# Sparse attention: item scores as three 64-row products a head, two heads on the two halves of the array

## The chip, the cores and the metric

The kernel runs on one core of a Trainium2 chip. The metric is device time in microseconds for one execution; shown are the times of several executions, and the profile of one of them. Engine names in the rows: PE is TensorE's matmuls, PEld its weight loads, DVE VectorE, ACT ScalarE, POOL GpSimd, SP SyncE, which issues the transfers.

## The reference

Two decoder layers over 512 tokens of width 1024: the first mixes tokens with latent attention (MLA), the second with the sparse attention in which the change lies. Each layer then attends to 256 memory tokens and applies a SwiGLU FFN; every part ends in a residual and a layer norm. The sparse attention, cut to what matters:

```python
h = x @ w_in        # q: 16 heads of 64, k and v: 4 heads of 64, q_idx: 8 of 64, k_idx: 64, w_idx: 8
def one_block(args):                                    # 128 queries
    dots = jnp.einsum('bqhd,bkd->bqhk', qi_blk, k_idx) * (IDX_DIM ** -0.5)
    score = jnp.einsum('bqh,bqhk->bqk', wi_blk, jax.nn.relu(dots))
    score = jnp.where(causal[None], score, -jnp.inf)
    _, sel = lax.top_k(score, topk)                     # topk = 128
    k_sel, v_sel, pos_sel = (gather_rows(a, sel) for a in (k, v, pos))
    logits = jnp.einsum('bqngd,bqknd->bqngk', qg, k_sel) * (DSA_HEAD_DIM ** -0.5)
    logits = jnp.where(sel_ok[:, :, None, None, :], logits + bias, -jnp.inf)
    p = jax.nn.softmax(logits, axis=-1)
    return jnp.einsum('bqngk,bqknd->bqngd', p, v_sel).reshape(b, Q_BLOCK, 1024)
out = from_blocks(lax.map(one_block, ...)) @ w_o
```

All of it is float32. The kernel reaches that precision with products of split operands: a value is a high part (rounded to TensorE's fp32r) and a low part, the rest.

## The kernel before

The kernel doesn't gather. For each query tile `qt` (128 queries, 0 to 3) it scores all keys up to the tile's end, n = 128 (qt + 1) of them, adds -2^100 to those that the top-k search has not chosen, and takes the softmax over the row. Matmuls are at least 256 columns wide, so N is 256, 256, 384 and 512 for the four tiles.

An ordinary projection (`mm3`, L126 to L128) is three products of 128 rows: high by high, high by low, low by high.

The item scores differ. A head has only 64 dimensions, so half the array's 128 rows would be empty. `stack_q_pool` (L942) therefore stacks the two parts of one head in the 128 rows. It gets the projection of two heads in one bank, copies it to SBUF as `f` (L944), casts the high part of the even head into rows 0 to 63 of `QA` and that of the odd head into rows 64 to 127 of `QB` (L945, L946, ScalarE), and GpSimd subtracts the low parts into the other half of each (L947, L948). The keys stand in both halves: `KA[g]` holds the high part of kv head g twice, `KB[g]` its low part twice. One product of `Q` with `KA` and one with `KB` (L1059, L1060) give all four part products of one head, accumulated in one bank. For tiles 1 to 3 a product with the identity (`identr`, L1058) first puts the mask of the top-k search into the bank.

`dsa_scores(qt, g)` does this for the four query heads of kv head g, one bank each, and hands each bank to VectorE (bias and row minimum, L428) and ScalarE (exponential, L435). `dsa_t` (L1072) turns the weights with four 128x128 transposes for each key block and splits them; `dsa_pv` multiplies them with the values (L1093, L1094), normalises (transposes at L1104) and stores the result. VectorE's top-k search (`topk`, L1004 and L1005) is spread between the query projections. Queries are projected for two heads at a time, j = 0 to 7; the scores of tile 0 are run between these projections by the table `steps`, those of the other tiles in a loop that keeps scores, turning and values of neighbouring items (qt, g) in flight. The scheduler then puts the instructions of each engine into their order; engines run their own lists in order and wait for each other by semaphores. Scores use the four banks "b", transposes and values the four banks "a".

Elsewhere in the kernel a score has the other form: the index scores (L984) take three products of 64 rows, one head on rows 0 to 63 and the next on rows 64 to 127, each into its own bank:

```python
pss = [bank("b") for _ in range(2)]
for a, b in ((0, KIA), (0, KIB), (1, KIA)):
    for e in range(2):
        es = slice(64 * e, 64 * e + 64)
        nc.tensor.matmul(pss[e][:, :n], qi[a][es, ts_], b[es, :n], start=b is KIA and a == 0, stop=a == 1)
```

Of the kernel before, what the change touches and what calls it, by code (L numbers as in the profile page):

```python
# [11 lines left out]
F32 = mybir.dt.float32  # L12
# [3 lines left out]
ALU = mybir.AluOpType  # L16
# [52 lines left out]
def tile_hybrid_mla_dsa_deepnorm_block(ctx: ExitStack, tc: tile.TileContext, A: dict, out: bass.AP):  # L69
    nc = tc.nc  # L70
# [9 lines left out]
    def nm(s):  # L80
        uid[0] += 1
        return f"{s}_{uid[0]}"

    def t2(dt=F32, shape=(P, 512)):
        return tp.tile(list(shape), dt, tag="t2", name=nm("t2"), bufs=39)
# [7 lines left out]
    def bank(tag, shape=(P, 512)):  # L93
        return pp.tile(list(shape), F32, tag=tag, name=nm("ps"))
# [17 lines left out]
    def chunk(src, shape, eng=None, after=(None, None)):  # L112
        n = int(np.prod(shape[1:]))
        raw = wp.tile([P, 1024], F32, tag="raw", name=nm("raw"), bufs=3)
        with behind(after[0]):
            nc.sync.dma_start(raw[:, :n], src)
        h = wp.tile([P, 1024], FR, tag="wh", name=nm("wh"))
        l = wp.tile([P, 1024], FR, tag="wl", name=nm("wl"))
        split(h[:, :n], l[:, :n], raw[:, :n], eng, after[1])
        if len(shape) == 2:  # L120
            return h[:, :n], l[:, :n]
        k = shape[1]
        return (h[:, :n].rearrange("p (k m) -> p k m", k=k), l[:, :n].rearrange("p (k m) -> p k m", k=k))
# [11 lines left out]
    identr = cp.tile([P, P], FR, name="identr")  # L135
# [273 lines left out]
    def proj_tiles(ws, XT, halves):  # L409
        pss = [bank("a") for _ in ws]  # L410
        if halves:
            for cols in HALVES:
                for ps, w in zip(pss, ws):
                    proj(ps, w, XT, cols)
        else:
            for ps, w in zip(pss, ws):
                proj(ps, w, XT, (0, 512))
        return pss
# [32 lines left out]
    def ts_of(tt):  # L451
        return slice(P * tt, P * tt + P)
# [46 lines left out]
    for c in range(4):  # L499
        h, l = XT[c // 2]  # L500
        rx = raw_x[c // 2]
        step = 1 if c == 0 else 2
        for i in range(0, 2, step):
            k0 = 2 * (c % 2) + i
            split(h[:, k0:k0 + step], l[:, k0:k0 + step], rx[:, k0:k0 + step])
            if 2 * c + i in w_parts:
                t, a, b = w_parts[2 * c + i]
                split(whs[t][:, a:b], wls[t][:, a:b], raw_w[t][:, a:b])
        for i in range(2):
            k = 2 * c + i  # L510
            xh, xl = k_of(XT, k)
            for tt in range(NT):
                ts_ = ts_of(tt)
# [60 lines left out]
    for tt in range(NT):  # L574
        ps = bank("a")
# [363 lines left out]
    XT = norm.XT  # L939


    def stack_q_pool(ps, QA, QB):  # L942
        f = t2()
        nc.scalar.copy(f, ps)  # L944
        nc.scalar.copy(QA[0:64], ps[0:64])  # L945
        nc.scalar.copy(QB[64:128], ps[64:128])  # L946
        nc.gpsimd.tensor_tensor(QA[64:128], f[0:64], QA[0:64].bitcast(F32), op=ALU.subtract)  # L947
        nc.gpsimd.tensor_tensor(QB[0:64], f[64:128], QB[64:128].bitcast(F32), op=ALU.subtract)  # L948

    wvs = [chunk(A["w_vi"][:, NV * k0:NV * k1], (P, k1 - k0, NV)) for k0, k1 in ((0, 3), (3, 6), (6, 8))]  # L950
    VD = t8(FR, (P, 4, 4, P))
# [2 lines left out]
    for tt in range(NT):  # L954
        pv = bank("a")
        ts_ = slice(P * tt, P * tt + P)
# [13 lines left out]
    masks = [None] + [t2() for _ in range(1, NT)]  # L970
    for j in range(4):
        pq = bank("a")
# [3 lines left out]
        for qt in range(1, NT):  # L976
            n = P * (qt + 1)
            ts_ = slice(P * qt, P * qt + P)
            acc = masks[qt]
# [6 lines that stand above are left out]
                h = 2 * j + e  # L986
# [12 lines left out]
    def topk(qt, its):  # L999
        n = P * (qt + 1)  # L1000
        acc = masks[qt]
        for it in its:
            m8 = tp.tile([P, 8], F32, tag="m8", name=nm("m8"), bufs=4)
            nc.vector.max(out=m8, in_=acc[:, :n])  # L1004
            nc.vector.match_replace(out=acc[:, :n], in_to_replace=m8, in_values=acc[:, :n], imm_value=-3e38)  # L1005
        if its[-1] < TOPK // 8 - 1:
            return
        mk = MK[:, qt]
        nc.vector.tensor_scalar(mk[:, :n], acc[:, :n], -2e38, -BIG, op0=ALU.is_gt, op1=ALU.mult)
        masks[qt] = mk  # L1010
# [3 lines left out]
    KA, KB = [], []  # L1014
# [15 lines left out]
    def dsa_bias(qt, g):  # L1030
        n = P * (qt + 1)
        c0 = 127 + 384 - 128 * qt
        if (qt, g) == (1, 0):
            bts = [t2(F32, (P, 2, 256)) for _ in range(2)]
        else:
            bts = [t8(F32, (P, 4, 512)) if qt else t2(F32, (P, 4, P))]
        m = 4 // len(bts)
        for i, bt in enumerate(bts):
            read = nc.sync.dma_start(bt[:, :, 0:n],
                                     scr[bass.ds(r * (1 + qt), 1), 4 * g + m * i:4 * g + m * i + m, :,  # L1040
                                         c0:c0 + n].rearrange("a h p k -> p (a h) k"))
        reads.append(read)
        return [bts[i // m][:, i % m, 0:n] for i in range(4)]

    Q, OTd = [], {}
    q8 = t8()
    first_bias, reads, spreads, copies = [], [], [], []

    def dsa_scores(qt, g):
        n = P * (qt + 1)  # L1050
        N = max(n, 256)
        ts_ = slice(P * qt, P * qt + P)
        bt = dsa_bias(qt, g) if 4 * qt + g > 4 else first_bias[4 * qt + g]
        sx = Softmax(bt)
        for i in range(4):
            ps = bank("b")
            if qt:
                nc.tensor.matmul(ps[:, :N], identr, masks[qt][:, :N], start=True, stop=False)  # L1058
            nc.tensor.matmul(ps[:, :N], Q[4 * g + i][:, ts_], KA[g][:, :N], start=qt == 0, stop=False)  # L1059
            nc.tensor.matmul(ps[:, :N], Q[4 * g + i][:, ts_], KB[g][:, :N], start=False, stop=True)  # L1060
            sx.exp(i, ps[:, :n], 0.125, bt[i], copies[-1] if copies else None)
        return sx

    def dsa_t(qt, g, sx):
# [54 lines left out]
    def run_s(i):  # L1119
        if i < 16:  # L1120
            Ss[i] = dsa_scores(*items[i])
# [7 lines left out]
    def run(word):  # L1129
        kind, i = word[0], int(word[1:])  # L1130
        if kind == "p":
            dsa_pv(*items[i], *PT.pop(i))
        else:
            (run_s if kind == "s" else run_t)(i)

    for j in range(8):
        if j < 5:
            first_bias.append(dsa_bias(j // 4, j % 4))
        for _ in range(min(NTK, len(todo))):
            topk(*todo.pop(0))  # L1140
        (pq,) = proj_tiles([chunk(A["w_q"][j], (P, NK, P), nc.gpsimd)], XT, False)
        if j < 2:
            qa, qb = q8[:, 2 * j], q8[:, 2 * j + 1]
        else:
            qa, qb = t2(FR), t2(FR)
        stack_q_pool(pq, qa, qb)
        Q += [qa, qb]
        for word in steps.get(j, "").split():
            run(word)

# [5 lines left out]
    for i in range(3, 16):  # L1156
        a = 1 if i < LA else 0
# [99 lines left out]
```

## Time and profile before

| | |
|---|---|
| time, median of 3 runs | 1523.58 us (1523.28 to 1525.23) |
| the profiled execution: its time, its span | 1523.23 us, 1521.4 us |
| busy share PE, DVE, ACT, POOL | 98%, 65%, 43%, 20% |
| index scores, L984 (72 products of 64 rows) | 788.8 to 812.7 us |
| query projections and their splits (L944 first to L948 last) | 832 to 881.4 us |
| item scores, L1059 and L1060 (128 products of 128 rows) | 843.9 to 941.0 us |

The span runs from the first to the last instruction of the profile; the time is the device's own and a little longer. A matmul's row in the timeline gives its start and its duration; neighbours overlap, so the durations of a busy stretch add up to more than the stretch. Rows of the form `out<-in 128*128 128x512` give the rows and columns of the stationary operand and the shape of the moving one; `64*128` is a product on 64 of the 128 rows. Line numbers are those of the kernel before.

### The profile page before, as it was taken

The numbers are of one execution on the slowest core, as the hardware profiler recorded it, in microseconds if no ns is written. First come the engines' busy times: TensorE is split into PE (matmuls) and PEld (weight loads), VectorE is DVE, ScalarE is ACT, GpSimd is POOL, SyncE is SP. The second block draws the span as 40 slices with busy tenths as digits, with TensorE's granted clock in tenths as the row PEclk, the third lists the DMA queues.
The fourth block names the chain that finished last, engine by engine and source line by source line (L and its number), as shares of the span: only waits on it lengthen the run. The fifth ranks groups of instructions, "written<-read, shape, count | busy, mean of one in ns | idle before, by whom it ended". The sixth has DMA issues, their size and how long they took to land.

```text
span 1521.4 us, 20268 instructions
## 1 busy us (share of the span) xinstructions
PE 1491.2 (98%) x7666; PEld 1263.9 (83%) x7666; DVE 992.5 (65%) x1735; ACT 647.2 (43%) x1156; POOL 304.2 (20%) x299
## 2 busy tenths in 40 slices
PE   9999999999999999999999989999999999999997
PEld 8788888988898888888888778898888888888886
DVE  7887868554746655654568989675557555666545
ACT  4777753443233333333256588344422433333320
POOL 1322001000032331410024653000002232323002
PEclk9999999999999999999999999999999999999999
DMA  6234423432333233333243146343423233232321
GB/s 216 72 104 116 143 83 133 128 115 70 126 97 98 83 125 98 97 97 98 91 139 96 60 160 225 111 139 97 122 72 125 83 125 97 97 104 78 99 95 56
DMA packets 51143, 166.16 MB, mean 109 GB/s; under 512 B 5284, under 2 KB 11828, under 8 KB 48996
## 3 DMA queue, kind: packets, MB, share of 16 engines
q1 hardware_dynamic: 50468, 163.61, 33.1%
q8 instruction: 60, 0.98, 0.3%
q10 hardware_dynamic: 576, 1.25, 0.2%
q14 instruction: 39, 0.32, 0.1%
HBM read 160.60 MB, written 9.47 MB: 112 GB/s over the span
## 4 chain that ended last, share of the span: by engine, by line
PE 86%; DVE 8%; ACT 3%; issue 2%; DMA 1%; POOL 0%; POOLq 0%; SPq 0%; DVEq 0%; ACTq 0%
PE ps L126 26%; PE ps L127 26%; PE ps L128 26%; DVE t L104 2%; DVE t L1005 2%; DVE m L1004 2%; ACT t L435 1%; PE ps L344 1%; PE ps L1072 1%; ACT t L102 1%; PE ps L660 1%; DVE wl L104 1%; PE ps L984 1%; PE ps L786 0%; PE ps L1093 0%
## 5 line engine op out<-in xcount | busy, mean ns | idle before, releaser
L126 PE MATMUL ps<-t,wh 128*128 128x512 f32 (+2 forms) x1248 | 452.1, 362 | 5.8 <-DVE t L104 3.4
L127 PE MATMUL ps<-t,wh 128*128 128x512 f32 (+2 forms) x1248 | 450.2, 361 | 1.2 <-DVE t L104 1.2
L128 PE MATMUL ps<-t,wl 128*128 128x512 f32 (+2 forms) x1248 | 450.5, 361 | 0.0
L102 ACT CAST wh<-raw 128x1024 fp32r<-128x1024 f32 (+2 forms) x217 | 226.5, 1044 | 438.0 <-PE ps L127 157.7
L104 DVE TENSOR_TENSOR wl<-raw,wh 128x1024 fp32r<-128x1024 f32 (+2 forms) x196 | 252.5, 1289 | 209.6 <-ACT wh L102 208.2
L126 PE MATMUL ps<-wh,t 128*128 128x512 f32 (+3 forms) x774 | 295.4, 382 | 0.0
L127 PE MATMUL ps<-wl,t 128*128 128x512 f32 (+3 forms) x774 | 293.2, 379 | 0.1
L128 PE MATMUL ps<-wh,t 128*128 128x512 f32 (+3 forms) x774 | 292.8, 378 | 0.0
L126 PEld LDWEIGHTS ps<-t,wh 128*128 128x128 f32 x1248 | 235.5, 189 | 43.1 <-DVE t L104 5.6
L128 PEld LDWEIGHTS ps<-t,wl 128*128 128x128 f32 x1248 | 235.6, 189 | 36.3 <-issue 1.1
L127 PEld LDWEIGHTS ps<-t,wh 128*128 128x128 f32 x1248 | 235.6, 189 | 35.9 <-DVE t L104 1.5
L102 ACT CAST t<-ps 128x512 fp32r<-128x512 f32 (+3 forms) x253 | 124.4, 524 | 130.2 <-PE ps L344 86.5
L128 PEld LDWEIGHTS ps<-wh,t 128*128 128x128 f32 x774 | 146.3, 189 | 25.9
L126 PEld LDWEIGHTS ps<-wh,t 128*128 128x128 f32 x774 | 146.5, 189 | 25.5 <-ACT t L435 0.4
L127 PEld LDWEIGHTS ps<-wl,t 128*128 128x128 f32 x774 | 146.3, 189 | 25.7 <-DVE wl L104 0.5
L287 POOL TENSOR_TENSOR sm<-sm,mhalf 128x1 f32<-128x1 f32 x32 | 30.1, 941 | 683.0 <-DVE sm L285 683.0
L104 DVE TENSOR_TENSOR t<-ps,t 128x512 fp32r<-128x512 f32 (+3 forms) x253 | 145.6, 606 | 27.0 <-ACT t L102 24.1
L102 ACT CAST wh<-t 128x1024 fp32r<-128x1024 f32 x56 | 58.9, 1052 | 141.8 <-PE ps L127 123.6
L104 DVE TENSOR_TENSOR wl<-t,wh 128x1024 fp32r<-128x1024 f32 x56 | 71.2, 1272 | 65.2 <-ACT wh L102 63.4
L889 DVE TENSOR_TENSOR t<-ps,t 128x512 f32<-128x512 f32 x44 | 30.4, 692 | 120.1 <-PE ps L128 120.1
L104 DVE TENSOR_TENSOR t<-t,t 128x512 fp32r<-128x512 f32 (+2 forms) x113 | 84.5, 751 | 28.0 <-ACT t L102 25.7
L102 ACT CAST t<-t 128x512 fp32r<-128x512 f32 (+2 forms) x113 | 64.5, 574 | 56.6 <-POOL t L823 33.3
(173 smaller groups left out, 1625.8 us busy)
## 6 DMA issues: line engine op xcount, KB each, us to landing
raw<-in_ffn_in_dram SPq DMA_DIRECT2D x88, 512.0 KB, 3.5
t<-in_ffn_dg_dram SPq DMA_DIRECT2D x16, 1024.0 KB, 5.1
raw<-in_xa_k_dram SPq DMA_DIRECT2D x16, 512.0 KB, 3.6
raw<-in_xa_v_dram SPq DMA_DIRECT2D x16, 512.0 KB, 3.6
raw<-in_xa_q_dram SPq DMA_DIRECT2D x16, 512.0 KB, 3.8
raw<-in_xa_o_dram SPq DMA_DIRECT2D x16, 512.0 KB, 3.5
raw<-in_ffn_dl_dram SPq DMA_DIRECT2D x12, 512.0 KB, 3.5
scr<-vscr SPq DMA_DIRECT2D x16, 319.5 KB, 4.5
```

The source lines that it names most:

```text
L102: nc.scalar.copy(h, src)
L104: low[0] = (eng or nc.vector).tensor_tensor(l, src, h.bitcast(F32), op=ALU.subtract)
L126: nc.tensor.matmul(ps, st[0], mv[0], start=start, stop=False, skip_group_check=more)
L127: nc.tensor.matmul(ps, st[0], mv[1], start=False, stop=False, skip_group_check=more)
L128: nc.tensor.matmul(ps, st[1], mv[0], start=False, stop=stop, skip_group_check=more)
L287: nc.gpsimd.tensor_tensor(b, a, mhalf, op=ALU.pow)
L344: nc.tensor.transpose(pt[:, k], x_of(tt)[:, 512 * n + P * k:512 * n + P * k + P], ident)
L435: nc.scalar.activation(Sx, src, AF.Exp, bias=nb, scale=scale, accum_out=self.sm[:, i:i + 1])
L660: nc.tensor.transpose(pt[:, P * qt:P * qt + P], Ss[qt][:, P * kb:P * kb + P], ident)
L889: nc.vector.tensor_tensor(sg, pu, sg, op=ALU.mult)
L1004: nc.vector.max(out=m8, in_=acc[:, :n])
L1005: nc.vector.match_replace(out=acc[:, :n], in_to_replace=m8, in_values=acc[:, :n], imm_value=-3e38)
```

## The change

The two parts of the queries are kept as they were projected: one tile with the high part of both heads (even head in rows 0 to 63, odd head in rows 64 to 127) and one with the low part. The scores of two heads are then three products of 64 rows each, high by high, high by low, low by high, the even head on the upper half of the array and the odd head on the lower, into two banks that are taken together; the product low by low is dropped. Behind the line of the change the same code stands five lines lower (L1072 is L1077, L1093 is L1098, L1104 is L1109); the mask product is L1058 in both, and the 64-row products are L1062.

```diff
-    def stack_q_pool(ps, QA, QB):
+    def split_pool(h, l, ps):
         f = t2()
+        nc.scalar.copy(h, ps)
         nc.scalar.copy(f, ps)
-        nc.scalar.copy(QA[0:64], ps[0:64])
-        nc.scalar.copy(QB[64:128], ps[64:128])
-        nc.gpsimd.tensor_tensor(QA[64:128], f[0:64], QA[0:64].bitcast(F32), op=ALU.subtract)
-        nc.gpsimd.tensor_tensor(QB[0:64], f[64:128], QB[64:128].bitcast(F32), op=ALU.subtract)
+        nc.gpsimd.tensor_tensor(l, f, h.bitcast(F32), op=ALU.subtract)
...
-        for i in range(4):
-            ps = bank("b")
+        for j in range(2):
+            q = Q[2 * g + j]
+            pss = [bank("b") for _ in range(2)]
             if qt:
-                nc.tensor.matmul(ps[:, :N], identr, masks[qt][:, :N], start=True, stop=False)
-            nc.tensor.matmul(ps[:, :N], Q[4 * g + i][:, ts_], KA[g][:, :N], start=qt == 0, stop=False)
-            nc.tensor.matmul(ps[:, :N], Q[4 * g + i][:, ts_], KB[g][:, :N], start=False, stop=True)
-            sx.exp(i, ps[:, :n], 0.125, bt[i], copies[-1] if copies else None)
+                for ps in pss:
+                    nc.tensor.matmul(ps[:, :N], identr, masks[qt][:, :N], start=True, stop=False)
+            for a, kt in ((0, KA[g]), (0, KB[g]), (1, KA[g])):
+                for e, ps in enumerate(pss):
+                    es = slice(64 * e, 64 * e + 64)
+                    nc.tensor.matmul(ps[:, :N], q[a][es, ts_], kt[es, :N],
+                                     start=qt == 0 and a == 0 and kt is KA[g], stop=a == 1)
+            for e, ps in enumerate(pss):
+                i = 2 * j + e
+                sx.exp(i, ps[:, :n], 0.125, bt[i], copies[-1] if copies else None)
...
-        stack_q_pool(pq, qa, qb)
-        Q += [qa, qb]
+        split_pool(qa, qb, pq)
+        Q.append((qa, qb))
```

Two places of TensorE's list show what this does to its order. In the names, `t_1545` holds the keys of kv heads 0 and 1, `t_1538` the masks of the top-k search, `t_1599` and `t_1600` query tiles, and `ps` numbers are banks as they are taken; `x4` are four alike.

TensorE, query tile 3, kv head 1, the second two heads, before:

```order
L1058 MATMUL ps_12173<-t_1538_10793,identr 128x512
L1059 MATMUL ps_12173<-t_1545_10831,t_1599_11100 128x512
L1060 MATMUL ps_12173<-t_1545_10831,t_1599_11100 128x512
L1072 MATMUL ps_12128<-ident,t_1851_11999 128x128 x4
L1058 MATMUL ps_12179<-t_1538_10793,identr 128x512
L1059 MATMUL ps_12179<-t_1545_10831,t_1600_11101 128x512
```

and after:

```order
L1058 MATMUL ps_12211<-t_1538_10793,identr 128x512
L1058 MATMUL ps_12212<-t_1538_10793,identr 128x512
L1062 MATMUL ps_12211<-t_1545_10831,t_1599_11094 128x512
L1062 MATMUL ps_12212<-t_1545_10831,t_1599_11094 128x512
L1062 MATMUL ps_12211<-t_1545_10831,t_1599_11094 128x512
L1062 MATMUL ps_12212<-t_1545_10831,t_1599_11094 128x512
L1062 MATMUL ps_12211<-t_1545_10831,t_1600_11095 128x512
L1062 MATMUL ps_12212<-t_1545_10831,t_1600_11095 128x512
L1077 MATMUL ps_12229<-ident,t_1873_12110 128x128 x4
```

Here the six products of a two-head group stand together, between mask products and transposes of 128 rows; the transposes that stood between the heads have moved behind them.

TensorE, query tile 2, kv head 1, the first two heads (value products L1093 or L1098, transposes L1072 or L1077 of an earlier item beside them), before:

```order
L1058 MATMUL ps_11847<-t_1538_10793,identr 128x384
L1059 MATMUL ps_11847<-t_1545_10831,t_1586_11044 128x384
L1060 MATMUL ps_11847<-t_1545_10831,t_1586_11044 128x384
L1072 MATMUL ps_11741<-ident,t_1747_11629 128x128 x4
L1058 MATMUL ps_11853<-t_1538_10793,identr 128x384
L1059 MATMUL ps_11853<-t_1545_10831,t_1587_11045 128x384
L1060 MATMUL ps_11853<-t_1545_10831,t_1587_11045 128x384
L1093 MATMUL ps_11750<-t_1757_11666,t_1451_10342 128x512
```

and after:

```order
L1062 MATMUL ps_11867<-t_1545_10831,t_1586_11040 128x384
L1098 MATMUL ps_11766<-t_1757_11678,t_1451_10342 128x512
L1099 MATMUL ps_11766<-t_1758_11679,t_1451_10342 128x512
L1098 MATMUL ps_11766<-t_1760_11687,t_1451_10342 128x512
L1099 MATMUL ps_11766<-t_1761_11688,t_1451_10342 128x512
L1109 MATMUL ps_11776<-ident,t_1754_11669 128x128 x2
L1077 MATMUL ps_11823<-ident,t_1767_11712 128x128 x4
L1062 MATMUL ps_11868<-t_1545_10831,t_1586_11040 128x384
L1062 MATMUL ps_11867<-t_1545_10831,t_1586_11040 128x384
L1062 MATMUL ps_11868<-t_1545_10831,t_1586_11040 128x384
L1062 MATMUL ps_11867<-t_1545_10831,t_1587_11041 128x384
L1077 MATMUL ps_11832<-ident,t_1767_11712 128x128 x4
```

Value products and transposes of 128 rows now stand inside the group of six: the first 64-row product is parted from the next four, and the sixth comes behind the last row.

## The prediction

> **What bounds the kernel now.** I read the page's busy table and its chain of waits first, then the windows around the changed code, then the waits of TensorE, and last the timeline matmul by matmul. From the page:
>
> ```profile
> PE 1491.2 (98%) x7666; PEld 1263.9 (83%) x7666; DVE 992.5 (65%) x1735; ACT 647.2 (43%) x1156; POOL 304.2 (20%) x299
> PE 86%; DVE 8%; ACT 3%; issue 2%; DMA 1%; POOL 0%; POOLq 0%; SPq 0%; DVEq 0%; ACTq 0%
> ```
>
> TensorE is the bound overall, so time added to it or taken from it counts, unless it lies where TensorE waits anyway. The changed code runs from 832 us (first query tile) to 941 us (last scores). Four windows of it (columns: length, then busy us of PE, PEld, DVE, ACT, POOL, then clock, DMA share, GB/s):
>
> ```profile
> 838.00:880.00 42.00, 36.81 (x182) 29.93 (x181) 40.49 (x119) 24.00 (x55) 26.81 (x27) 1.00 0.25 81
> 880.00:893.00 13.00, 11.07 (x63) 9.10 (x64) 8.77 (x36) 9.47 (x31) 5.51 (x9) 0.87 0.02 6
> 893.00:914.00 21.00, 19.59 (x119) 16.25 (x118) 19.12 (x64) 19.67 (x53) 11.85 (x23) 1.00 0.65 225
> 914.00:941.00 27.00, 27.00 (x151) 22.10 (x150) 25.54 (x72) 23.13 (x56) 11.10 (x26) 1.00 0.77 273
> ```
>
> I call them A, B, C, D. In A the vector engine is the full one (40.49 of 42 us, the top-k search) and TensorE has gaps. B is a hand-over between engines. C is shared by ScalarE, VectorE and TensorE. In D, the scores of query tile 3, TensorE is never idle. The waits of TensorE say the same (two of A, one of B, one of C, the only one after 914):
>
> ```profile
> PE ps L1104 <- POOL t L440: 1.4, 1, 1.4
> PE ps L126 <- ACT t L946: 1.1, 1, 1.1
> PE ps L1059 <- DVE sm L428: 2.2, 1, 2.2
> PE ps L1093 <- DVE t L1101: 1.1, 2, 0.9
> PE ps L1072 <- DVE t L1101: 0.2, 1, 0.2
> ```
>
> **Price of a full-array product.** Successive matmuls overlap, so what one costs is the distance to the next start, not its duration. From the timeline (columns: start, duration):
>
> ```profile
> 906.54 0.34 PE L1059 MATMUL ps<-t,t 128*128 128x384 f32 x1
> 906.71 0.34 PE L1060 MATMUL ps<-t,t 128*128 128x384 f32 x1
> ...
> 925.04 0.40 PE L1059 MATMUL ps<-t,t 128*128 128x512 f32 x1
> 925.27 0.39 PE L1060 MATMUL ps<-t,t 128*128 128x512 f32 x1
> 925.51 0.60 PE L1072 MATMUL ps<-ident,t 128*128 128x128 f32 x4
> 925.86 0.48 PE L1058 MATMUL ps<-t,identr 128*128 128x512 f32 x1
> 926.17 0.40 PE L1059 MATMUL ps<-t,t 128*128 128x512 f32 x1
> ```
>
> Steps are 0.174 us at 384 columns and 0.231 at 512. Four transposes and the product behind them take 926.17 - 925.51 = 0.66 us: 0.231 for the product and 0.107 for each transpose, with whatever the change from one to the other costs already in it. At 256 columns the chain of waits gives 0.12:
>
> ```profile
> 894.11 0.12 PE ps L1058
> 894.23 0.12 PE ps L1059
> ```
>
> **Price of 64-row pairs.** The kernel already has this form in the item index scores (L984), in the middle of 128-row projections:
>
> ```profile
> 795.40 0.33 PE L126 MATMUL ps<-t,wh 128*128 128x384 f32 x1
> 795.57 0.34 PE L127 MATMUL ps<-t,wh 128*128 128x384 f32 x1
> 795.91 0.39 PE L984 MATMUL ps<-t,t 64*128 64x256 f32 x2
> 796.13 0.46 PE L984 MATMUL ps<-t,t 64*128 64x256 f32 x3
> 798.20 0.39 PE L984 MATMUL ps<-t,t 64*128 64x512 f32 x1
> 798.53 0.45 PE L128 MATMUL ps<-t,wl 128*128 128x384 f32 x1
> 798.81 0.34 PE L126 MATMUL ps<-t,wh 128*128 128x384 f32 x1
> 798.99 0.33 PE L127 MATMUL ps<-t,wh 128*128 128x384 f32 x1
> ```
>
> The x2 row is a pair: two products in 0.39 us, the time of one, so the halves do run together. But the last 128-row product before the pairs (795.57) holds the next start off for 0.34 us instead of 0.17: the pair starts when that product has ended (795.57 + 0.34 = 795.91), where 128-row products overlap. The first pair takes 0.22 to the next start instead of 0.12. On the way out the last 64-row product takes 0.33 instead of 0.23, and the first 128-row one 0.28 instead of 0.17. Excess: 0.16 + 0.10 + 0.10 + 0.11 = 0.47 us for one visit from 128 rows to 64 and back. That is the term on which this prediction rests.
>
> [...]
>
> **The change part by part.**
>
> 1. Products. Two heads took four products of N columns and now take three pair steps, so one step per two heads is saved where pairs hold. Counted over the changed order: 8 two-head groups for each query tile; where the order splits a pair, or puts both products of one half next to each other, a single costs a whole step. Tile 2: 32 steps before, 27 now, saved 5 x 0.174 = 0.87 us. Tile 3: 32 before, 26 now, 6 x 0.231 = 1.39 us. 256 columns (tiles 0 and 1): 64 before, 56 now, 8 x 0.12 = 0.96 us.
>
> 2. Visits. The mask products, the transposes and the value products stay 128 rows wide and stand between the groups, and the order cuts groups further, as shown above for tile 2. Counted: 16 visits at 256 columns, 19 in tile 2, 13 in tile 3. At 0.47 us: 7.5, 8.9 and 6.1 us. TensorE's work thus grows by 6.5, 8.1 and 4.7 us.
>
> 3. What of it lies on the path, window by window.
>  A: 4 visits of tile 0 and the first 2 of tile 1. TensorE has the waits of 1.4, 1.1 and 2.2 us shown above here, and the top-k search on VectorE runs on to 879 us whatever TensorE does. I cost it at 0. If that cover fails (VectorE is in order: a softmax step that waits for late scores holds up the search behind it), 6 x 0.47 less 7 steps saved is 2.0 us.
>  B: 6 visits against 3 steps saved, +2.5 us of TensorE, partly under a run of exponentials that ScalarE works off back to back; the wait for the last query tile gets shorter (next item). I take +1, between 0 and +2.5.
>  C: the last group of tile 1 (4 visits, and two steps lost to split pairs: 2.1 us) and tile 2 (8.1 us): +10.2 us. TensorE's cover there, by counts times steps:
>
> ```profile
> L1072 PE MATMUL ps<-ident,t 128*128 128x128 f32 x38 | 6.0, 279 | 0.4 <-DVE t L1101 0.2
> L1058 PE MATMUL ps<-t,identr 128*128 128x384 f32 x15 | 5.8, 384 | 0.0
> L1093 PE MATMUL ps<-t,t 128*128 128x512 f32 x8 | 3.4, 423 | 1.2 <-DVE t L1101 1.1
> L1104 PE MATMUL ps<-ident,t 128*128 128x128 f32 x8 | 1.5, 272 | 0.0
> L1058 PE MATMUL ps<-t,identr 128*128 128x256 f32 x4 | 1.2, 303 | 0.0
> ```
>
>  (L1059 and L1060 have L1058's counts, L1094 has L1093's.) 46 x 0.107 + 45 x 0.174 + 16 x 0.231 + 12 x 0.12 = 17.9 us of 21, so 3 us of slack. Some of it stays, since a chain that goes through three engines keeps some waits; I let 2 be eaten: +8.
>  D: TensorE is idle for 0.2 us only: +4.7 whole. Behind it follow projections bound by TensorE, so nothing is given back.
>  16 of the 36 visits in C and D end at a transpose, a way out for which there is no row: between the 0.20 us of a product and nothing, 0 to -3.2 in all. I take -0.8, near the row of the product, since a transpose is 128 rows wide as well.
>
> 4. The query split. ScalarE does two copies of the bank instead of three casts or copies, and GpSimd one subtraction of 128 rows instead of two of 64:
>
> ```profile
> 875.92 0.58 ACT L944 COPY t<-ps 128x512 f32<-128x512 f32 x1 [2.06 <-PE ps L128]
> 876.40 0.58 ACT L945 CAST t<-ps 64x512 fp32r<-64x512 f32 x1
> 877.01 0.58 ACT L946 CAST t<-ps 64x512 fp32r<-64x512 f32 x1
> L947 POOL TENSOR_TENSOR t<-t,t 64x512 fp32r<-64x512 f32 x8 | 10.4, 1303 | 3.3 <-ACT t L945 2.7
> L948 POOL TENSOR_TENSOR t<-t,t 64x512 fp32r<-64x512 f32 x8 | 10.3, 1290 | 0.6
> ```
>
>  A copy of 128 rows costs what a cast of 64 does, 0.58, so ScalarE is spared one of 0.58 per tile and GpSimd one of 1.29 us. Both engines are behind VectorE in A, so this shows only at the last tile, where TensorE waits at 880: a gain between 0 and 1.3 us, already netted in B's +1. Bank release after a projection comes at most 0.5 us earlier, under the same cover.
>
> Sum: A 0, B +1, C +8, D +4.7, ways out -0.8 = +13 us. On the profiled execution's 1523.23 us (its span is 1521.4) this gives 1536.2; the median of the runs, 1523.58, is 0.35 above it. I say 1536.
>
> **The rivals.**
>
> *The switch costs nothing and the kernel gets faster.* The 0.47 us would then belong to the index scores (waits for a bank or for the low half) and not to the form. Only the saved steps count: tile 3's 1.39, some 0.9 in C and up to 1.3 from the query split, 1523.2 - 3.6 = 1520. It decides below 2.0 us saved over the 36 visits of C and D, 0.056 us a visit. Against it: the excess at entry is exactly the overlap that 128-row products have. [...]
>
> *Switching next to a transpose is free.* 16 entries and 16 exits of C and D are at transposes; without 16 x 0.26 + 16 x 0.20 the sum is +5.6, 1529. No row shows 64 rows next to a transpose; the transposes are 128 rows wide too, which speaks against it.
>
> *Pairs fall out of step.* Two heads need two banks at once, and a late bank makes one half run behind: in the index scores the 18 products from 795.91 to 798.53 take 2.62 us where nine steps (three of each width) are 1.57, and the switch explains 0.2 of the 1.05 between them. Were the remaining 0.28 a group lost in each of the 18 groups of C and D, 1541.
>
> *Waits swallow it.* If C and D are paced by ScalarE and VectorE after all (VectorE is 25.54 of 27 us in D), about 1524; the 0.2 us of idle TensorE in D speaks against it.
>
> **How the numbers follow.** My forecast, 1531 to 1539, gets 0.62; free switches 0.07; free next to transposes 0.12; out of step, 1539 to 1545, 0.14; swallowed 0.05. The range 1527 to 1543 holds the forecast and most of the second and third rival: it reaches down to A and B gaining and the 0.47 being smaller at transposes, and up to all 19.3 us of added work. A measurement of this kernel can tell about 0.2%, 3 us, from no change. Faster by that: 0.06 (free switches, most of it). Within it: 0.07. Slower: 0.87.
>
> **What would show it.** In the profile after, the first 64-row product behind a mask product should start about 0.34 us (384 columns) or 0.39 (512) after it, and the first 128-row one behind a visit should be followed after 0.28 to 0.34. The stretch from 914 to the last scores should be some 31 to 32 us instead of 27, and C some 8 longer; A should end within 1 us of before. If starts in a pair differ by a whole step, the third rival holds. The forecast is wrong if the stretches of one query tile are not longer than before.

## The result and the profile after

The changed kernel takes 1538.36 us (median of 4 runs, 1535.78 to 1538.84), the kernel before 1523.81 (1523.28 to 1525.23) in runs on the same chip: a ratio of 1.0091, with a 95% interval from 1.0073 to 1.0108. It is 14.5 us slower; 1536, within 1527 to 1543, was forecast. The profiled execution took 1538.20 us, with a span of 1536.4.

The page after, busy times and the shares of the chain of waits:

```profile
PE 1507.4 (98%) x7730; PEld 1265.1 (82%) x7730; DVE 994.6 (65%) x1735; ACT 643.1 (42%) x1148; POOL 293.5 (19%) x291
PE 86%; DVE 9%; ACT 2%; issue 2%; DMA 1%; POOL 0%; POOLq 0%; SPq 0%; DVEq 0%; ACTq 0%
```

TensorE stays the bound, with 16 us more of busy time; ScalarE and GpSimd do less, as the shorter query split says. The four windows of the prediction, now (columns: length, busy us of PE, PEld, DVE, ACT, POOL, clock, DMA share, GB/s):

```profile
838.00:880.00 42.00, 40.22 (x200) 31.34 (x198) 40.40 (x117) 20.12 (x48) 16.89 (x19) 0.96 0.22 66
880.00:893.00 13.00, 10.64 (x52) 7.69 (x51) 8.59 (x37) 7.46 (x28) 1.76 (x3) 0.74 0.22 78
893.00:914.00 21.00, 19.46 (x113) 13.05 (x113) 15.00 (x50) 15.38 (x40) 14.28 (x24) 1.00 0.43 144
914.00:941.00 27.00, 26.94 (x149) 17.48 (x148) 21.56 (x60) 19.63 (x48) 9.33 (x22) 1.00 0.66 227
```

Here the clock of the second window stands out: 0.74, where it was 0.87. Otherwise the windows no longer hold the same work, since the later parts have moved; and the profiled execution was already 1.3 us later at the index scores, in code that is the same. So the traces are cut at five events that both have: the last index score, the end of the top-k search, the first scores of tile 2, those of tile 3, and the first transpose of the norm behind the attention (L344). Same columns, before:

```profile
812.30:883.30 71.00, 65.55 (x309) 53.61 (x307) 67.27 (x205) 42.80 (x91) 40.27 (x36) 0.99 0.28 90
883.30:895.60 12.30, 10.63 (x70) 8.79 (x69) 8.86 (x37) 8.53 (x29) 6.72 (x13) 0.95 0.13 40
895.60:916.60 21.00, 19.59 (x114) 16.04 (x113) 19.09 (x59) 19.84 (x51) 11.26 (x23) 1.00 0.62 209
916.60:984.20 67.60, 67.48 (x346) 55.20 (x345) 53.35 (x122) 38.30 (x86) 10.96 (x24) 1.00 0.53 186
```

and after:

```profile
813.60:883.60 70.00, 66.24 (x313) 52.26 (x310) 66.97 (x192) 34.94 (x72) 29.73 (x28) 0.98 0.29 91
883.60:904.00 20.40, 18.48 (x99) 13.14 (x98) 10.99 (x51) 13.44 (x46) 8.54 (x13) 0.83 0.19 65
904.00:928.50 24.50, 24.50 (x135) 15.74 (x134) 20.15 (x61) 20.34 (x51) 11.98 (x23) 1.00 0.54 177
928.50:999.10 70.60, 69.92 (x357) 52.98 (x356) 52.78 (x118) 36.41 (x81) 8.42 (x22) 1.00 0.47 166
```

The four stretches go from 71.0, 12.3, 21.0 and 67.6 us to 70.0, 20.4, 24.5 and 70.6: -1.0, +8.1, +3.5 and +3.0, together 171.9 to 185.5, +13.6. From there to the end of the span both take the same, 537 us. The longest piece of it, 8.1 us, lies between the top-k search and tile 2, not in tile 2.

A visit to 64 rows in tile 3, from the timeline of after (columns: start, duration; an x2 row is a pair):

```profile
942.46 0.40 PE L1058 MATMUL ps<-t,identr 128*128 128x512 f32 x1
942.79 0.50 PE L1062 MATMUL ps<-t,t 64*128 64x512 f32 x2
943.13 0.39 PE L1062 MATMUL ps<-t,t 64*128 64x512 f32 x2
943.36 0.39 PE L1062 MATMUL ps<-t,t 64*128 64x512 f32 x2
943.68 0.50 PE L1058 MATMUL ps<-t,identr 128*128 128x512 f32 x1
944.02 0.40 PE L1058 MATMUL ps<-t,identr 128*128 128x512 f32 x1
944.35 0.50 PE L1062 MATMUL ps<-t,t 64*128 64x512 f32 x2
```

A step between products of 512 columns is 0.23 us. Here the mask product takes 0.33 to the first pair, the first pair 0.34, the second 0.23, the third 0.32 and the first mask product behind the visit 0.34: an excess of 0.10 + 0.11 + 0 + 0.09 + 0.11 = 0.41 us. Over all visits at full clock the medians of the starts give 0.39 to 0.40 where a product follows and 0.35 where transposes follow (the first transpose takes 0.06 longer, not 0.11); 256, 384 and 512 columns are alike. The two products of a pair start 0.003 us apart by the median.

What TensorE waited for in after, and the longest stretch in which its clock was halved:

```profile
PE ps L1062 <- DVE sm L428: 2.4, 2, 2.0
PE ps L1077 <- ACT t L435: 1.1, 1, 1.1
PE ps L1077 <- DVE t L104: 0.9, 1, 0.9
...
885.30:892.10 6.80, 6.80 (x28) 4.93 (x27) 2.69 (x17) 4.79 (x20) 0.00 (x0) 0.50 0.01 2
```

Of the first row 2.0 us are the wait ahead of tile 0's last scores, which ends at 883.3 us. Two microseconds later TensorE runs at half clock for 6.8 us. Before, the same wait (2.2 us) stood in the same place, ended at 880.0, and was followed by a half-clock stretch of 3.4 us:

```profile
881.20:884.60 3.40, 3.16 (x14) 3.07 (x15) 2.61 (x13) 3.40 (x16) 0.18 (x1) 0.50 0.00 0
```

### The profile page after: what moved, and what is told of

The parts are those of the page before. It is cut to its first block, busy times and chain, and to the rows that moved or that the text cites. A ratio compares the mean times of both kernels' runs of the same rounds, so it can differ in the third digit from the quotient of the medians.

```text
span 1536.4 us, 20368 instructions
## 1 busy us (share of the span) xinstructions
PE 1507.4 (98%) x7730; PEld 1265.1 (82%) x7730; DVE 994.6 (65%) x1735; ACT 643.1 (42%) x1148; POOL 293.5 (19%) x291
## 4 chain that ended last, share of the span: by engine, by line
PE 86%; DVE 9%; ACT 2%; issue 2%; DMA 1%; POOL 0%; POOLq 0%; SPq 0%; DVEq 0%; ACTq 0%
PE ps L126 26%; PE ps L127 26%; PE ps L128 26%; DVE t L1003 2%; DVE t L104 2%; DVE m L1002 2%; PE ps L1062 1%; PE ps L1077 1%; PE ps L344 1%; PE ps L1058 1%; PE ps L1098 1%; DVE wl L104 1%; ACT t L435 1%; PE ps L1099 1%; PE ps L660 1%
## 5 line engine op out<-in xcount | busy, mean ns | idle before, releaser
L104 DVE TENSOR_TENSOR wl<-raw,wh 128x1024 fp32r<-128x1024 f32 (+2 forms) x196 | 252.5, 1289 | 212.7 <-ACT wh L102 211.5
L128 PEld LDWEIGHTS ps<-wh,t 128*128 128x128 f32 x774 | 146.4, 189 | 26.1
L104 DVE TENSOR_TENSOR t<-ps,t 128x512 fp32r<-128x512 f32 (+3 forms) x253 | 145.2, 606 | 29.3 <-ACT t L102 25.2
L104 DVE TENSOR_TENSOR wl<-t,wh 128x1024 fp32r<-128x1024 f32 x56 | 71.2, 1272 | 65.2 <-ACT wh L102 63.4
L104 DVE TENSOR_TENSOR t<-t,t 128x512 fp32r<-128x512 f32 (+2 forms) x113 | 84.8, 753 | 28.1 <-ACT t L102 25.9
L435 ACT ACTIVATE t<-t,sm 128x128 f32<-128x128 f32 (+3 forms) x128 | 71.0, 556 | 45.3 <-DVE sm L428 45.0
```

The lines of the kernel that those rows point to most:

```text
L104: low[0] = (eng or nc.vector).tensor_tensor(l, src, h.bitcast(F32), op=ALU.subtract)
L128: nc.tensor.matmul(ps, st[1], mv[0], start=False, stop=stop, skip_group_check=more)
L435: nc.scalar.activation(Sx, src, AF.Exp, bias=nb, scale=scale, accum_out=self.sm[:, i:i + 1])
```

## The experiments

**The price of a visit by itself.** Two kernels put one extra product ahead of 80 projections of the feed-forward part of the kernel before, where TensorE is never idle (busy 50.00 of 50.00 us from 1200 to 1250) and everything around is 128 rows wide. The projection that follows overwrites it. One has 128 rows (the control), the other 64:

```diff
+    nc.tensor.matmul(ps, w[0][0:64, 0], k_of(XT, 0)[0][0:64], start=True, stop=True)
     proj(ps, w, XT, (0, 512))
```

The control was expected to do:

> The kernel before, with one more product of 128 rows and 512 columns ahead of each of 80 FFN projections (into the same bank, overwritten by the projection's first product). Control for the next run. Both theories: 80 x 0.227 us = +18 us, about 1542.

and the kernel with 64 rows:

> The kernel before, with one more product of 64 rows (the upper half of the array) ahead of the same 80 projections: 80 visits from 128 rows to 64 and back, away from the sparse attention and its waits. Theory (the switch itself costs 0.40 us: in the trace after 0.09 at entry, 0.11 for the first 64-row step, 0.09 at exit, 0.11 for the first 128-row step): 80 x 0.40 = 32 us above the control, about 1574. Rival (the excess belongs to waits of the attention code, not to the form): the control's time within 2 us.

The control took 1542.24 us (ratio 1.0116, 1.01 to 1.0131; before 1523.88), 18.4 us for 80 products, a step of 0.23 each. The kernel with 64 rows took 1573.26 (1.0325, 1.031 to 1.0341). The 31.0 us between them are (1573.26 - 1542.24) / 80 = 0.388 us for a visit. The timeline of the latter:

```profile
1221.72 0.39 PE L127 MATMUL ps<-t,wh 128*128 128x512 f32 x1
1221.95 0.39 PE L128 MATMUL ps<-t,wl 128*128 128x512 f32 x1
1222.27 0.50 PE L913 MATMUL ps<-t,wh 64*128 64x512 f32 x1
1222.70 0.50 PE L126 MATMUL ps<-t,wh 128*128 128x512 f32 x1
1223.03 0.39 PE L127 MATMUL ps<-t,wh 128*128 128x512 f32 x1
1223.26 0.39 PE L128 MATMUL ps<-t,wl 128*128 128x512 f32 x1
```

Steps of 0.23, 0.32, 0.43, 0.33 and 0.23: the same 0.09 in, 0.20 on the single product (the first one's and the last one's share fall together) and 0.10 behind. The price belongs to the form, not to banks, low parts or the order of this kernel's attention.

**The same order without the switch.** This kernel has after's list of TensorE, instruction by instruction, with the score products on all 128 rows:

```diff
-                    nc.tensor.matmul(ps[:, :N], q[a][es, ts_], kt[es, :N],
+                    nc.tensor.matmul(ps[:, :N], q[a][:, ts_], kt[:, :N],
```

> The changed kernel with the same list of TensorE, instruction by instruction, but its 192 score products on all 128 rows, so that there is no switch and nothing runs together (each score then sums two heads; the output is another one). Theory: the loss lies in the 48 switches of 0.35 to 0.40 us. Against them stand whole steps for halves that ran together: 21 more of 0.174 in tile 2 and 22 of 0.229 in tile 3. So tile 2 (24.5 us from its first score to tile 3's) falls by 19 x 0.38 - 3.7 = 3.5 to about 21, tile 3 onwards stays within 1 us of 70.6 (13 x 0.38 - 5.0 = -0.1), and the first part (tiles 0 and 1) gains 1 to 3: 1531 to 1535. Rival (late banks and the new order are the loss, and the halves save what they should): at least the whole steps come on top, 1545 or more.

It took 1530.89 us (ratio 1.0048, 1.0034 to 1.0062; before 1523.60), 7.5 less than after (6.6 by the two ratios), though none of the 192 score products has a partner any more and TensorE takes a whole step for each. Its four stretches:

```profile
813.90:883.90 70.00, 65.48 (x313) 53.31 (x310) 66.97 (x192) 34.82 (x72) 29.77 (x28) 1.00 0.28 91
883.90:899.50 15.60, 14.08 (x97) 11.88 (x97) 10.72 (x49) 11.83 (x41) 7.33 (x13) 1.00 0.14 45
899.50:921.40 21.90, 21.74 (x136) 19.31 (x135) 20.21 (x63) 20.72 (x54) 12.31 (x23) 1.00 0.63 216
921.40:991.60 70.20, 70.02 (x357) 57.68 (x355) 52.80 (x118) 37.17 (x82) 9.42 (x24) 1.00 0.50 171
```

Tile 2 by counts: 48 steps instead of 27 cost 21 x 0.174 = 3.7 us, and 19 visits that are gone free 7.1; that is -3.4, and -2.6 was measured. Tile 3: 22 x 0.231 = 5.1 us against 4.8 for 13 visits, so +0.3, and -0.4 was measured. The second stretch falls by 4.8, where 1 to 3 had been forecast for tiles 0 and 1; its clock is 1.00, so this holds the gain from the clock as well as that from the visits. In this trace the steps into and out of a run of score products exceed the plain step by 0.00 us (medians), where after has 0.09 and 0.09: the same order with the same neighbours, and the price is gone with the 64 rows.

**The order of the two heads' products.** Instead of alternating, the three products of the even head come first, then the three of the odd one:

```diff
-            for a, kt in ((0, KA[g]), (0, KB[g]), (1, KA[g])):
-                for e, ps in enumerate(pss):
-                    es = slice(64 * e, 64 * e + 64)
+            for e, ps in enumerate(pss):
+                es = slice(64 * e, 64 * e + 64)
+                for a, kt in ((0, KA[g]), (0, KB[g]), (1, KA[g])):
```

> The changed kernel, with the three products of the even head first and then the three of the odd one, so that the halves no longer run together (51 visits instead of 48). Theory that pairs do run together in the changed kernel: some 22 steps of 0.23 us more in tile 3, 21 of 0.17 in tile 2, 20 of 0.12 in tile 1, +9 to +12 us, about 1549. Rival (pairs fall out of step anyway): within 3 us of the changed kernel's 1538.

It took 1541.65 us (1.0112, 1.0096 to 1.0127), 3.3 more than after and not 9 to 12: a miss. Its trace says why. At one place of tile 3 TensorE's list has two products of the even head (bank 12128) and then three of the odd (12129):

```
L1109 MATMUL ps_1872_12102<-ident_69,t2_1836_11976 128x128 x2
L1062 MATMUL ps_1878_12128<-t8_1545_10831,t8_1553_10886 128x512 x2
L1062 MATMUL ps_1879_12129<-t8_1545_10831,t8_1553_10886 128x512 x3
```

The timeline there:

```profile
936.30 0.27 PE L1109 MATMUL ps<-ident,t 128*128 128x128 f32 x1
936.50 0.50 PE L1062 MATMUL ps<-t,t 64*128 64x512 f32 x2
936.84 0.40 PE L1062 MATMUL ps<-t,t 64*128 64x512 f32 x2
937.08 0.39 PE L1062 MATMUL ps<-t,t 64*128 64x512 f32 x1
```

Five products in three steps, not five. Products of one half follow each other by a whole step (in after the second and third of one head start at 900.75 and 900.87 us, 0.12 apart at 256 columns; here the steps are 0.34 and 0.24), so each x2 row holds one of each head: the odd head's first product, third in the list, starts with the even head's first of the two, ahead of the other. The semaphores of the trace say the same: the product that ends the even head's sum, second in the list, is the one that counts a semaphore up, and the one that does so starts at 936.84. Not every pair is found so: in tiles 2 and 3 36 and 31 steps were counted, after needs 27 and 26, and without any pairing it would be 48 and 48. So this run doesn't price a lost pair, as it was meant to; it shows that the halves repaired much of a bad order here.

**The query split as before.** The changed scores, with two copies of 64 rows on ScalarE and two subtractions of 64 rows on GpSimd:

```diff
-        nc.scalar.copy(h, ps)
...
-        nc.gpsimd.tensor_tensor(l, f, h.bitcast(F32), op=ALU.subtract)
+        for s in (slice(0, 64), slice(64, 128)):
+            nc.scalar.copy(h[s], ps[s])
+        for s in (slice(0, 64), slice(64, 128)):
+            nc.gpsimd.tensor_tensor(l[s], f[s], h[s].bitcast(F32), op=ALU.subtract)
```

> The changed kernel, with the query split in as many instructions as before (three on ScalarE, two on GpSimd, each half of the rows by itself). Theory that the cheaper split is hidden behind the top-k search: 1538 within 1 us. Rival that it gave back time at the last query tile: +1 to +2 us, about 1540.

It took 1535.88 us (1.0078, 1.0064 to 1.0091; after's interval overlaps), 2.5 less than after, so it missed "within 1 us", to the side away from the rival. From the last index score to the first norm transpose it takes 185.4 us, after 185.5; of the 3.4 us by which its profiled execution is ahead, 2.8 were there at the last index score, before the changed code began. The shorter split brings nothing that can be seen.

**The clock.** Ten products of 512 columns that nothing uses are put in the wait ahead of tile 0's last scores, held there by an order on TensorE, in the changed kernel and in the one before:

```diff
     run_s(4)
+    fl = bank("a")
+    for _ in range(10):
+        with behind(pel[0]):
+            filled = nc.tensor.matmul(fl, identr, KA[0], start=True, stop=True)
+    pel[0] = filled
     run_s(3)
```

The changed kernel with them:

> The changed kernel with the same ten unused products at the same place, after which its trace shows a granted clock of 0.5 for 6.8 us (885 to 892). Theory that the lower clock is a part of the loss: the stretch goes away and 2.5 to 3.4 us come back, about 1535.5. Rival (the stretch from the end of the search to tile 2 is longer by its visits and waits alone): 1538 within 1 us, at full clock.

and the kernel before with them:

> The kernel before, with ten unused products of 512 columns (2.3 us) in the wait of TensorE ahead of the last scores of tile 0, after which the trace shows a granted clock of 0.5 for 3.4 us. If the clock stays full, 1 to 1.7 us faster, about 1522.5; if the stretch is paced by ScalarE anyway, the same time within 0.5 us.

The second stretch (end of the top-k search to tile 2) of each, first the changed kernel, then the one before:

```profile
882.00:899.60 17.60, 15.71 (x100) 10.76 (x98) 10.86 (x51) 13.20 (x46) 8.53 (x13) 1.00 0.21 76
```

```profile
883.60:897.70 14.10, 11.13 (x74) 9.03 (x75) 9.72 (x42) 9.81 (x34) 6.61 (x13) 1.00 0.11 31
```

In both the clock is 1.00. The changed kernel fell to 1534.47 us (1.0076, 1.0064 to 1.0088); the kernel before stayed at 1523.71 (1.0001, 0.9992 to 1.001), where 1522.5 had been forecast if the clock stayed full. The gain of the changed kernel is 3.9 us by the medians and 2.3 by the ratios, whose intervals overlap. Its six executions differ: four took 1533.1 to 1534.8 us at a mean granted clock of 0.996 to 0.997, the other two 1537.1 and 1538.5 at 0.995, which are after's numbers (0.994 to 0.996). So the ten products do not keep the clock full each time, and what follows holds for the profiled executions. Up to tile 2, the first two stretches together, before takes 83.3 us and 83.5 with full clock in the second, after 90.4 and 87.6. So the change costs 4.1 us there at full clock, and the clock adds 3.0. The wait alone is not the cause: without the switch the same wait was 2.4 us long, and the clock stayed at 1.00.

```profile
PE ps L1062 <- DVE sm L428: 2.4, 1, 2.4
```

**Fewer visits.** All four heads of a group together: four masks, then the score products in one run, held so from tile 1 on by an order on TensorE through the transposes and value products. That leaves 25 visits in place of 48: 4 instead of 19 in tile 2 and 4 instead of 13 in tile 3. One kernel does it with 64-row pairs, its control with the stacked 128-row products of before:

```diff
-        for j in range(2):
...
-            pss = [bank("b") for _ in range(2)]
+        pss = [bank("b") for _ in range(4)]
+        with behind(pel[0] if qt else None):
...
+            for j in range(2):
...
+                        pel[0] = nc.tensor.matmul(ps[:, :N], q[a][es, ts_], kt[es, :N],
```

The pairs were expected to do:

> The changed kernel, with TensorE kept in program order from query tile 1 on: four mask products, then the twelve 64-row products of a kv head, then transposes and values of other items, so 25 visits instead of 48 (4 instead of 13 in tile 3, 4 instead of 19 in tile 2) and no split pairs. Theory (visits cost 0.35 to 0.40 us each): 23 x 0.38 and 5 x 0.2 us of steps are 10 us less than the changed kernel if the order costs no new waits, about 1528. Rival (the time lies in late banks and in the order of waits, not in visits): no better than 1537, since this order overlaps less.

and the control:

> The kernel before in the same program order (four mask products, then eight stacked products of a kv head): what the order alone costs. Theory of visits: the pair form in this order is slower by 25 x 0.38 less some 25 saved steps (4.5 us), +5 us, of which about half hidden in tiles 0 and 1: grouped_pairs is 2 to 5 us above this run instead of 14.5. Rival (late banks or the clock make the difference): the gap stays above 8 us.

The pairs took 1551.21 us (1.0176, 1.0163 to 1.0189; before 1523.14), the control 1541.32 (1.0112, 1.0098 to 1.0127). The forecast of about 1528 for the pairs was a miss by 23 us: the order alone, with 128 rows, costs 18. Waits of TensorE from 880 us on, first the pairs (L1104 and L1118 are the value product and the transpose behind it):

```profile
PE ps L1118 <- DVE t L104: 7.0, 4, 2.6
PE ps L1104 <- DVE t L104: 6.7, 3, 3.1
PE ps L1065 <- DVE sm L428: 3.2, 1, 3.2
```

and the control's:

```profile
PE ps L1116 <- DVE t L104: 5.6, 4, 1.4
PE ps L1102 <- DVE t L104: 5.0, 3, 2.6
PE ps L1078 <- DVE t L1112: 3.0, 2, 2.4
```

A strict order takes from TensorE the other work that it would do while VectorE works through the banks (L104 is the subtraction that makes the low parts). With it goes a lower clock: the stretch ahead of tile 2, first the pairs, then the control:

```profile
882.10:910.30 28.20, 24.67 (x113) 18.35 (x113) 15.76 (x61) 18.57 (x55) 10.30 (x18) 0.70 0.21 72
```

```profile
883.60:905.60 22.00, 16.01 (x84) 13.45 (x84) 13.41 (x48) 15.73 (x45) 10.25 (x18) 0.82 0.34 120
```

The pairs are 9.9 us behind their control, where visits and steps saved would give 2 to 5; 6.2 of it is this stretch, with its clock of 0.70. By the two expectations it is the rival that came out, a gap above 8 us. So the pair does not say what fewer visits are worth. In tile 2 and from tile 3 on the gap between the forms shrinks from 3.5 and 3.0 us to 2.1 (28.2 against 26.1) and 1.5 (73.6 against 72.1), the direction that fewer visits should give, but under other waits and clocks; nothing more is claimed.

## Why the prediction was right, and where it was not

The sum was 13 us and 13.6 were measured where the code is changed. The mechanism holds: 64-row products between 128-row ones cost TensorE more in changes of form than their pairs save (by counts 18.2 us against 3.2), and TensorE is the bound. But its terms were off, and they cancelled: up to tile 2 it was 4.0 us too low, in tile 2 2.6 too high and from tile 3 on 1.7 too high, with -0.8 for the ways out beside them. That the sum came out within 1 us is luck; that the kernel gets slower, by visits, is not.

- **The price of a visit**, 0.47 us: too high. It is 0.39 to 0.40 in after, 0.388 measured alone. The part that was off is the entry, 0.16 in all four visits of the index scores and 0.09 by the medians of after and of the kernel with 80 visits; the other three, 0.10, 0.10 and 0.11, were 0.11, 0.09 and 0.11. What held up the index scores' entry by another 0.07 is open. By visits this is (32 x 0.395 + 16 x 0.35) = 18.2 us, against 48 x 0.47 - 0.8 = 21.8.
- **The ways out at transposes**, -0.8 in all: 0.05 each over 16, 0.8. This was right.
- **The steps saved**: pairs held, with starts 0.003 us apart, and 27 and 26 steps in tiles 2 and 3 as counted. (The prediction called the 0.39 us of an x2 row the time of one product; a single one of 256 columns lasts 0.28 in the kernel before, so it is the starts that show the pair.)
- **A at 0**: the stretch up to the end of the top-k search became 1.0 us shorter. The cover held, even with a half-clock stretch of 3.4 us from 854.5 on, behind TensorE's wait of 1.1 us for L435. The search goes on longer than the prediction read: its last step starts at 883.3 us in the kernel before, not at 879.
- **B at +1** and tile 1's last group at 2.1, 3.1 together: 7.1 were measured up to tile 2. At full clock it is 4.1; the other 3.0 are the clock, for which the prediction had no term, though its own row of B showed 0.87. This is the largest error: the hand-over ahead of tile 2 was priced with a clock that stays as it was.
- **C**: tile 2 was put at 8.1 less 2 of slack. Its 19 visits cost 8 x 0.35 + 11 x 0.395 = 7.1 us and 0.9 of steps are saved, and 3.5 were measured. So some 2.7 us went into TensorE's slack, of which nothing is left (PE busy 24.50 of 24.50). The price was too high and the slack that is eaten too low.
- **D at 4.7**: 3.0 were measured from the first scores of tile 3 to the first norm transpose. At the price found, 13 visits cost 6 x 0.395 + 7 x 0.35 = 4.8 us; less 1.4 for six steps this is 3.4. The scores alone, from the first start to the last, take 29.1 us instead of 24.0, much like the sign that the prediction named. But by itself this length does not tell what made it: the kernel with the same list and no switch takes 29.1 as well, with 22 more whole steps (5.1 us) in place of the visits.
- **The query split**, a gain of 0 to 1.3 within B: 0.1 (185.4 against 185.5). Hidden.

The rivals. *The switch costs nothing* (1520) falls: 0.388 us a visit where nothing else differs. Inside a visit the two products of a pair do start 0.003 us apart; the price lies on the way in and out. *Free next to a transpose* (1529) falls too: from transposes into 64 rows the visit costs as much as from products (the last transpose takes 0.20 us instead of 0.107, 0.10 more, where a product takes 0.09 more), and out to transposes 0.05 less. *Out of step* (1541) is not seen in after, and in the kernel with the heads one after the other the halves found each other again. *Swallowed by waits* (1524) was true up to the end of the search and for some 2.7 us in tile 2, not beyond.

Of the signs that were named, the first 64-row product came 0.33 us behind a mask product at 512 columns instead of 0.39, since the entry was too dear; the first 128-row product behind a visit was followed after 0.34 there, within the 0.28 to 0.34 given.

What stays open: why the half-clock stretch of after was 6.8 us and that of before 3.4. It is not one execution's chance: the kernel with the query split as before has a clock of 0.84 over its 21.1 us from the end of the search to tile 2 (after has 0.83 over 20.4), an estimate of 21.1 x 0.16 / 0.5 = 6.8 us at half clock. In the profiled executions, filling the wait removes it and taking the switch away removes it too, but the strict order without any 64-row score has a lower clock there as well (0.82 in its row). What decides it was not tried.

## What to carry to other kernels

By these prices, products on half the rows can pay only when many stand together: three pairs of 512 columns save one step of 0.23 us against four stacked products and cost 0.39 for each visit from 128 rows and back, so by this estimate one visit must hold at least two two-head groups here before it gains, and at 384 and 256 columns three and four. No run here shows such a gain. Count visits in the order that the engine's list really has, with the masks, transposes and value products in it, and try the form with the order unchanged before forcing an order: holding products together by hand cost 18 us here. Where TensorE's clock is already below 1 in a stretch, a change that adds work there is to be priced with the clock, and a few idle products in the wait show what it is worth (2.8 us up to tile 2 here, in the execution in which they kept the clock full, and nothing in the kernel before).

## What the runs showed of the hardware that was not expected

- Products on the two halves of the rows started out of the list's order in the kernel with the heads one after the other: five products, two of one half and then three of the other, began at 936.50, 936.50, 936.84, 936.84 and 937.08 us. That the engines run their own lists in order, as is said of the kernel before, does not hold for TensorE there.
- The change of form is paid in four places, 0.09, 0.11, 0.09 and 0.11 us, at 256, 384 and 512 columns alike, and a single product carries both middle ones (0.20). The price here is 0.39 us there and back (0.388 by itself).
- Transposes of 128 rows next to 128-row products cost no such change: what the last transpose saves (-0.08 us) the product behind it takes longer (+0.08), in the kernel before.
